# DeltaNet preparation with its mask additions on VectorE, two Gb buffers, and the scan's decay masks loaded and made step by step

## The chip, the cores and the metric

The kernel runs on one core of a Trainium2 chip. The metric is the time of one execution on the device in microseconds (us); lower is better. Beside the times there is one profiled execution, whose trace has every instruction of the engines: TensorE (PE, with its weight loads PEld), VectorE (DVE), ScalarE (ACT), GpSimd (POOL), and SyncE (SP), which issues the DMA loads and stores.

## The reference, cut to what matters

One layer over 512 latent tokens and a context of 256, width 1024: attention and a gated DeltaNet side by side, both projected from one input product, merged by gates, then a gated MLP. The change is in the DeltaNet (8 heads of width 128, two directions, chunked):

```python
gam = jnp.cumsum(log_a, axis=-1)
dec = jnp.exp(jnp.where(incl, gam[..., :, None] - gam[..., None, :], -jnp.inf))
kk = jnp.einsum('bhncd,bhnsd->bhncs', k, k)
a_mat = jnp.where(strict, beta[..., :, None] * dec * kk, 0.0) + jnp.eye(GDN_CHUNK)
uw = lax.linalg.triangular_solve(a_mat, rhs, left_side=True, lower=True, unit_diagonal=True)
...
p = dec * jnp.einsum('bhncd,bhnsd->bhncs', q, k)
...
delta = u_c - jnp.einsum('bhcd,bhde->bhce', w_c, s)
s_new = gl_c[..., None, None] * s + jnp.einsum('bhcd,bhce->bhde', kd_c, delta)
o = jnp.einsum('bhcd,bhde->bhce', qd_c, s) + jnp.einsum('bhcs,bhse->bhce', p_c, delta)
```

The matrix `dec` is needed twice: strictly triangular, times k k^T, in the triangular system; with its diagonal, times q k^T, in the scan's output. It is always made in the same way: the cumulative decays gam are broadcast from DRAM to all partitions, a mask of large numbers is added so that the excluded half vanishes in the exponential, and ScalarE takes the exponential with the token's own gam as bias.

## The kernel before, in words

The kernel works in chunks of 128 tokens, six to a head (two of the context, four latent), and takes the heads in four pairs, p = 0 to 3. For each pair there are three parts:

- `gdn_prep(p)` (L874 to L900) loads kT, makes the scale gT, and makes NN, which holds for each of the pair's two heads (hh) six masked decay matrices of both directions: per head one load of 6 x 128 numbers to all partitions into NN (direction 0) and one into Gb (direction 1), a mask addition to each (L895 by its call of `tt`; the helper's line in the trace is L108), six exps to each on ScalarE (L120), and the addition NN + Gb. For pair 0 these additions are on VectorE, for pairs 1 to 3 on GpSimd. Gb has one buffer, so the load for the second head starts when the first head's NN + Gb is done.
- `gdn_solve` (L902) has PE multiply k by k (`pk`), VectorE multiply that into NN, transposes blocks of 32 into C and X, and runs a triangular inversion of 31 steps, each a product `prod` and an addition into R. These 62 operations are on VectorE for pair 0 and on GpSimd for pairs 1 to 3. VectorE then scales R by gT and transposes it into o_tr and o_nt. `gdn_inv` (L943) builds the full inverse TTm from these with PE, VectorE (copies Y and TTm) and GpSimd.
- `gdn_scan(p)` (L1011 to L1118) walks through six steps in both directions: PE multiplies k by the state S, VectorE makes the remainder r, PE multiplies r by TTm, VectorE copies the result to dl, ScalarE scales it to dk, PE and VectorE update S. `decay_mask(c)` makes the scan's decay matrix M of latent chunk c: four loads of 128 x 128 (64 KB, L1023), two mask additions on GpSimd of 128 x 256, four exps on ScalarE. `intra(c)`, at the end of steps 1 to 4, multiplies M by the product q k^T (`pqk`). The scan makes all four masks in one line ahead of its first step; the tag M2 has four buffers.

The solve and the inverse of pair p + 1 are interleaved with the inverse and the scan of pair p. Between these, PE works through `filler()`, the input projections, whose accumulations (`mb`) VectorE and ScalarE move out of PSUM into `t` and `co`; weights are split in two parts, `whi` on ScalarE and `wlo` on VectorE, for products in three passes. `weave` deals out so many pieces of filler per step of the DeltaNet. The order of PE's matmuls is kept as written (`keep_in_program_order` while `pinned` holds). On the other engines and in the DMA queue a scheduler sets the order: by priorities (`sooner`, `solver`, `first`, `early`) and by when an instruction's inputs and buffers are there in its own model. Each engine then carries out its instructions strictly in that order, so one that waits holds all behind it. By the scheduler's order, loads of M of pair 0, which by the code come in the scan, may stand ahead of the loads of Gb of the same pair's preparation.

Of the kernel before, what the change touches and what calls it, by code (L numbers as in the profile page):

```python
# [6 lines left out]
F32 = mybir.dt.float32  # L7
F32R = mybir.dt.float32r
AF = mybir.ActivationFunctionType
ALU = mybir.AluOpType  # L10
# [4 lines left out]
P = 128  # L15
D = 1024
# [40 lines left out]
WB = 3  # L57
P0 = 1
GL = 4
# [19 lines left out]
def hybrid_layer_body(tc, x, ctxt, xT, consts, cols, rows, w_mod1, w_mod2, w_db, w_aq, w_cm, w_pa, w_pd, w_out,  # L79
# [54 lines left out]
    with es:  # L134
# [738 lines left out]

        def gdn_prep(p, eng=G):  # L874
            kT = gq.tile([P, 2, NA], F32, name="kT", tag="kT", bufs=2)
# [13 lines left out]
            for hh in range(2):  # L889
                u = slice(6 * hh, 6 * hh + 6)  # L890
                Gb = gq.tile([P, 6, P], F32, name="Gb", tag="Gb", bufs=1)
                for d, D in ((0, NN[:, u, :]), (1, Gb)):
                    r0 = d * 48 + p * 12 + hh * 6
                    SP.dma_start(D.rearrange("p a b -> p (a b)"),
                                 gamdr[r0:r0 + 6, :].rearrange("a b -> (a b)").partition_broadcast(P))  # L895
                    tt(D, D, msk_s[d].unsqueeze(1).to_broadcast([P, 6, P]), ALU.add, eng)
                    for c in range(6):
                        act(D[:, c, :], D[:, c, :], AF.Exp, scale=-1.0, bias=gam[:, r0 + c:r0 + c + 1])
                tt(NN[:, u, :], NN[:, u, :], Gb, ALU.add, eng)
            return [kT, gT, NN]  # L900
# [110 lines left out]
        def gdn_scan(p, pre, seqs):  # L1011
# [7 lines left out]
            def decay_mask(c):  # L1019
                M2 = gpool[0].tile([P, 2, 2, P], F32, name="M2", tag="M2", bufs=4)  # L1020
                for d in range(2):
                    for hh in range(2):
                        SP.dma_start(M2[:, d, hh, :], gamdr[cidx(d, hh, c), :].partition_broadcast(P))  # L1023
                    tt(M2[:, d], M2[:, d], msk_i[d].unsqueeze(1).to_broadcast([P, 2, P]), ALU.add, G)
                    for hh in range(2):
                        kc = cidx(d, hh, c)
                        act(M2[:, d, hh, :], M2[:, d, hh, :], AF.Exp, bias=ngam[:, kc:kc + 1])
# [10 lines left out]

            masks = {c: decay_mask(c) for c in (4, 3, 5, 2)}
            PTs = {}  # L1040
            for st in range(6):
                lat = st >= 2
                if st == 2:
                    oacc = gpool[0].tile([P, 2, 4, P], F32, name="oacc", tag="oacc")
# [138 lines left out]
        with early():  # L1183
            pre = gdn_prep(0, V if P0 else G)
        pas_es, y_es, yt = ExitStack(), ExitStack(), []
# [398 lines left out]
```

## Time and profile before

| | us |
|---|---|
| median of 3 runs | 1303.81 |
| lowest and highest | 1303.12, 1305.67 |
| profiled execution | 1306.96 |
| its span | 1304.3 |

The span is the time from the first to the last instruction of the profiled execution, whose own time is 2.7 us longer. Busy times are given as shares of the span, TensorE's granted clock as a share of full speed (0.978 over the span). A row of the timeline gives the start and the duration of an instruction (or of several like it in a row, with xcount), its engine, line, operation and tiles (out<-in), and in square brackets the idle time of the engine just before and what ended it. A row of the groups by line gives the count, the busy time, the mean duration in ns and the idle time before them. Preparation, solve and scan of the four pairs lie between 350 and 850 us of the span: pair 0's preparation at 350 to 412, scan 0 beside solve 1 at 460 to 545, scan 1 beside solve 2 at 560 to 640, scan 2 beside solve 3 at 640 to 725, scan 3 at 745 to 850.

### The profile page before, as it was taken

What the parts mean: (1) busy time and instruction counts of PE and PEld (TensorE: products, weight loads), DVE (VectorE), ACT (ScalarE), POOL (GpSimd) and SP (SyncE); (2) the same over time, 40 slices, a digit from 0 to 9 for tenths busy, and PEclk for the clock granted to TensorE, in tenths of its full rate; (3) what the DMA queues carried; (4) which work ended last, traced back from release to release, by engine and by line L of the source; (5) the groups of instructions that cost most, each with busy time, mean ns of one, the idle gap of its engine ahead of it and who ended that gap; (6) DMA issues with size and microseconds to landing.
All of it is one profiled execution on the core that took longest, in us unless ns stands there. A gap on an engine that the chain in (4) does not pass through costs nothing.

```text
span 1304.3 us, 20850 instructions
## 1 busy us (share of the span) xinstructions
PE 1229.6 (94%) x7835; PEld 1031.3 (79%) x7835; DVE 848.4 (65%) x1625; ACT 626.3 (48%) x1403; POOL 308.3 (24%) x364
## 2 busy tenths in 40 slices
PE   7899999999968999899998999999999999999997
PEld 4487878999857877778787878788988888888886
DVE  5886987777759986685665556555576666663323
ACT  5453656666576665474453443233354444443221
POOL 1752420000143249559447300000000000000000
PEclk8999999999998999899999999999999999999998
DMA  8656631121373342543533555265043222233331
GB/s 321 227 169 197 223 118 62 65 86 50 111 252 105 124 140 91 177 131 110 178 120 116 170 165 168 92 219 190 9 129 97 97 97 95 91 94 97 90 100 65
DMA packets 70789, 170.80 MB, mean 131 GB/s; under 512 B 7872, under 2 KB 18720, under 8 KB 69280
## 3 DMA queue, kind: packets, MB, share of 16 engines
q1 hardware_dynamic: 70688, 169.47, 39.4%
q8 instruction: 61, 1.00, 0.3%
q14 instruction: 40, 0.33, 0.1%
HBM read 144.23 MB, written 25.21 MB: 130 GB/s over the span
## 4 chain that ended last, share of the span: by engine, by line
PE 66%; POOL 10%; DVE 9%; DMA 5%; ACT 4%; issue 3%; SPq 0%; POOLq 0%; DVEq 0%; ACTq 0%
PE mc L87 32%; PE mb L87 17%; PE pq L87 4%; POOL R L108 4%; POOL prod L108 4%; PE pb L87 3%; PE pS L87 3%; PE ab L87 2%; PE ab L91 1%; DMA Gb<-gamdr 1%; PE xb L91 1%; DVE wlo L108 1%; PE pk L87 1%; DMA sz<-gdr 1%; POOL NN L108 1%
## 5 line engine op out<-in xcount | busy, mean ns | idle before, releaser
L108 DVE TENSOR_TENSOR wlo<-wraw,whi 128x1024 fp32r<-128x1024 f32 x152 | 187.6, 1235 | 162.6 <-ACT whi L120 161.6
L120 ACT ACTIVATE whi<-wraw 128x1024 fp32r<-128x1024 f32 x152 | 159.1, 1048 | 205.5 <-PE mc L87 106.5
L87 PE MATMUL mb<-hxH,whi 128*128 128x512 f32 x384 | 165.1, 430 | 2.1 <-DVE R L108 1.9
L87 PE MATMUL mb<-hxL,whi 128*128 128x512 f32 x384 | 155.0, 404 | 0.0
L87 PE MATMUL mb<-hxH,wlo 128*128 128x512 f32 x384 | 154.3, 402 | 0.0
L87 PE MATMUL mc<-h2L,whi 128*128 128x512 f32 (+1 forms) x376 | 142.7, 379 | 0.0
L87 PE MATMUL mc<-h2H,whi 128*128 128x512 f32 (+1 forms) x376 | 142.3, 378 | 0.3 <-ACT whi L120 0.3
L87 PE MATMUL mc<-h2H,wlo 128*128 128x512 f32 (+1 forms) x376 | 140.8, 374 | 0.5 <-DVE wlo L108 0.5
L108 POOL TENSOR_TENSOR rc<-rc,mhalf 128x2 f32<-128x2 f32 x4 | 3.3, 818 | 459.4 <-DVE rc L114 459.4
L87 PEld LDWEIGHTS mb<-hxH,wlo 128*128 128x128 f32 x384 | 74.0, 193 | 18.3
L87 PEld LDWEIGHTS mb<-hxH,whi 128*128 128x128 f32 x384 | 74.6, 194 | 13.9 <-ACT t L120 2.1
L87 PEld LDWEIGHTS mb<-hxL,whi 128*128 128x128 f32 x384 | 74.6, 194 | 10.3
L87 PEld LDWEIGHTS mc<-h2H,whi 128*128 128x128 f32 x376 | 70.6, 188 | 14.9 <-ACT whi L120 0.5
L87 PEld LDWEIGHTS mc<-h2H,wlo 128*128 128x128 f32 x376 | 70.6, 188 | 14.7 <-DVE wlo L108 1.0
L87 PEld LDWEIGHTS mc<-h2L,whi 128*128 128x128 f32 x376 | 70.7, 188 | 12.2
L87 PE MATMUL mc<-aH,whi 128*128 128x512 f32 (+1 forms) x198 | 72.9, 368 | 0.6 <-DVE x L117 0.6
L87 PE MATMUL mc<-aL,whi 128*128 128x512 f32 (+1 forms) x198 | 73.0, 369 | 0.0
L87 PE MATMUL mc<-aH,wlo 128*128 128x512 f32 (+1 forms) x198 | 72.0, 364 | 0.0
L117 DVE SCALAR_TENSOR_TENSOR u<-mc,col,u 128x511 f32<-128x511 f32 x88 | 65.3, 746 | 1.4
L108 POOL TENSOR_TENSOR prod<-X,R 128x31 f32<-128x31 f32 (+15 forms) x93 | 53.5, 576 | 22.3 <-DVE X L108 15.4
L108 POOL TENSOR_TENSOR R<-R,prod 128x31 f32<-128x31 f32 (+15 forms) x93 | 57.1, 613 | 6.8
L87 PE MATMUL pq<-whi,hxH 128*128 128x256 f32 x192 | 56.6, 295 | 0.0
(354 smaller groups left out, 3078.3 us busy)
## 6 DMA issues: line engine op xcount, KB each, us to landing
wraw<-in_w_cm_dram SPq DMA_DIRECT2D x48, 512.0 KB, 3.9
wraw<-in_w_up_dram SPq DMA_DIRECT2D x44, 512.0 KB, 3.7
wmd<-in_w_mod_dram SPq DMA_DIRECT2D x64, 256.0 KB, 3.8
wm<-in_w_mod_dram SPq DMA_DIRECT2D x8, 1024.0 KB, 8.2
wraw<-in_w_down_dram SPq DMA_DIRECT2D x16, 512.0 KB, 3.5
wraw<-in_w_aq_dram SPq DMA_DIRECT2D x12, 512.0 KB, 4.8
M<-gamdr SPq DMA_DIRECT2D x64, 64.0 KB, 4.4
wraw<-in_w_pa_dram SPq DMA_DIRECT2D x8, 512.0 KB, 4.0
```

Of the source, the lines that this page charges most:

```text
L87: i = nc.tensor.matmul(*a, **k)
L91: i = nc.tensor.transpose(*a, **k)
L108: (eng or V).tensor_tensor(out=out, in0=a, in1=b, op=op)
L117: V.scalar_tensor_tensor(out=out, in0=a, scalar=s, in1=b, op0=op0, op1=op1)
L120: A.activation(out, a, f, **kw)
```

## The change

In `gdn_prep` all mask additions and NN + Gb are on VectorE, for all pairs, and Gb gets a second buffer. In `decay_mask` the loads and the two additions keep their places in the order of the code (`late_op`), and the additions are on VectorE instead of GpSimd. The scan no longer makes four masks ahead of its first step: each of its steps 0 to 3 makes one at its head, for use at the end of the step behind it.

```diff
-P0 = 1
...
-        def gdn_prep(p, eng=G):
+        def gdn_prep(p):
...
-                Gb = gq.tile([P, 6, P], F32, name="Gb", tag="Gb", bufs=1)
+                Gb = gq.tile([P, 6, P], F32, name="Gb", tag="Gb", bufs=2)
...
-                    tt(D, D, msk_s[d].unsqueeze(1).to_broadcast([P, 6, P]), ALU.add, eng)
+                    tt(D, D, msk_s[d].unsqueeze(1).to_broadcast([P, 6, P]), ALU.add)
...
-                tt(NN[:, u, :], NN[:, u, :], Gb, ALU.add, eng)
+                tt(NN[:, u, :], NN[:, u, :], Gb, ALU.add)
...
-                        SP.dma_start(M2[:, d, hh, :], gamdr[cidx(d, hh, c), :].partition_broadcast(P))
-                    tt(M2[:, d], M2[:, d], msk_i[d].unsqueeze(1).to_broadcast([P, 2, P]), ALU.add, G)
+                        late_op(SP.dma_start(M2[:, d, hh, :], gamdr[cidx(d, hh, c), :].partition_broadcast(P)))
+                    late_op(V.tensor_tensor(out=M2[:, d], in0=M2[:, d], in1=msk_i[d].unsqueeze(1).to_broadcast([P, 2, P]), op=ALU.add))
...
-            masks = {c: decay_mask(c) for c in (4, 3, 5, 2)}
-            PTs = {}
+            masks, PTs = {}, {}
+            late_op = tc.keep_in_program_order
             for st in range(6):
                 lat = st >= 2
+                if st < 4:
+                    c = (4, 3, 5, 2)[st]
+                    masks[c] = decay_mask(c)
...
-            pre = gdn_prep(0, V if P0 else G)
+            pre = gdn_prep(0)
```

PE's order of instructions stays as it is. Lines behind L58 have a number smaller by one in the changed kernel up to the scan. On SP, in the preparation of pair 0, the loads of Gb and of the scan's masks M (M_5591 to M_5624 are pair 0's four masks), wraw (weights) and parts of the projections stood so before:

```order
L1023 DMA M_5591<-gamdr 128x128 x4
L1023 DMA M_5602<-gamdr 128x128 x3
L197 DMA wraw<-in_w_cm_dram 128x1024
L1023 DMA M_5602<-gamdr 128x128
L1023 DMA M_5613<-gamdr 128x128 x3
L894 DMA Gb<-gamdr 128x768
L1023 DMA M_5613<-gamdr 128x128
L1023 DMA M_5624<-gamdr 128x128 x4
L197 DMA wraw<-in_w_cm_dram 128x1024
L305 DMA vtd_133<-co 128x768
L894 DMA Gb<-gamdr 128x768 x2
```

The loads of NN and Gb at the same place of the changed kernel, from the first one on:

```order
L893 DMA NN<-gamdr 128x768
L893 DMA Gb<-gamdr 128x768
L893 DMA NN<-gamdr 128x768
L893 DMA Gb<-gamdr 128x768
L876 DMA kT<-kTd_107 128x768
L876 DMA kT<-kTd_108 128x768
L893 DMA NN<-gamdr 128x768 x2
L304 DMA ktd_126<-co 128x768
L196 DMA wraw<-in_w_cm_dram 128x1024
L893 DMA Gb<-gamdr 128x768 x4
```

The second Gb of pair 0 has moved ahead to the first; the loads of M are gone from here and stand some 20 rows further down, in the first scan, where those of all four masks of pair 0 stand close together.

VectorE's order in the same stretch, before (NN<-NN,cst and Gb<-Gb,cst are mask additions, co and t are the filler's, NN<-NN,pk is the product with k k^T):

```order
L108 TENSOR_TENSOR NN<-NN,Gb 128x768
L117 SCALAR_TENSOR_TENSOR co<-co,t_4310 128x768
L117 SCALAR_TENSOR_TENSOR t_4399<-mb,col,t_4399 128x511 x2
L108 TENSOR_TENSOR NN<-NN,pk 128x512
L108 TENSOR_TENSOR NN<-NN,pk 128x256
L108 TENSOR_TENSOR wlo<-wraw,whi 128x1024
L117 SCALAR_TENSOR_TENSOR t_4399<-mb,col,t_4399 128x255
L108 TENSOR_TENSOR Gb<-Gb,cst 128x768
L117 SCALAR_TENSOR_TENSOR t_4399<-mb,col,t_4399 128x255
L108 TENSOR_TENSOR NN<-NN,Gb 128x768
```

And in the changed kernel, from the second row on of the same place:

```order
L107 TENSOR_TENSOR NN<-NN,cst 128x768
L107 TENSOR_TENSOR g<-g,rkk_176 128x6 x2
L107 TENSOR_TENSOR NN<-NN,cst 128x768
L107 TENSOR_TENSOR NN<-NN,Gb 128x768
L116 SCALAR_TENSOR_TENSOR co<-co,t_4310 128x768
L107 TENSOR_TENSOR Gb<-Gb,cst 128x768
L116 SCALAR_TENSOR_TENSOR t_4399<-mb,col,t_4399 128x511
L107 TENSOR_TENSOR Gb<-Gb,cst 128x768
L116 SCALAR_TENSOR_TENSOR t_4399<-mb,col,t_4399 128x511
L107 TENSOR_TENSOR NN<-NN,pk 128x512
L107 TENSOR_TENSOR NN<-NN,Gb 128x768
L107 TENSOR_TENSOR NN<-NN,pk 128x256
```

Pair 1's additions to NN stand ahead of co, and its additions to Gb ahead of the product with pk; pair 0's own Gb is no longer here, being done earlier. Five to seven rows further down pair 2's two additions to Gb stand ahead of the last product with pk.

The third place is on VectorE where the solve of pair 1 begins, beside the opening of pair 0's scan (Y is a part of `gdn_inv`, C and X are the solve's). Before:

```order
L986 COPY Y_0_4243<-pb 64x384
L117 SCALAR_TENSOR_TENSOR co<-tz,mb 128x512
L108 TENSOR_TENSOR NN<-NN,pk 128x512
L986 COPY Y_1_4244<-pb 64x384
L108 TENSOR_TENSOR NN<-NN,pk 128x256
L919 STREAM_TRANSPOSE C<-NN 32x12x32 x4
L923 STREAM_TRANSPOSE X<-C 128x1024
```

And in the changed kernel:

```order
L985 COPY Y_0_4243<-pb 64x384
L116 SCALAR_TENSOR_TENSOR co<-tz,mb 128x512
L107 TENSOR_TENSOR NN<-NN,pk 128x512
L1023 TENSOR_TENSOR M_5591<-M_5591,cst 128x256
L985 COPY Y_1_4244<-pb 64x384
L107 TENSOR_TENSOR NN<-NN,pk 128x256
L1023 TENSOR_TENSOR M_5591<-M_5591,cst 128x256
L918 STREAM_TRANSPOSE C<-NN 32x12x32 x4
L1023 TENSOR_TENSOR M_5656<-M_5656,cst 128x256 x2
L922 STREAM_TRANSPOSE X<-C 128x1024
```

Four mask additions of pair 0's scan have come in between the copies of Y, C and X.

## The prediction

> **What bounds the kernel now.** The page comes first: the busy times, then the chain that ended last.
>
> ```profile
> PE 1229.6 (94%) x7835; PEld 1031.3 (79%) x7835; DVE 848.4 (65%) x1625; ACT 626.3 (48%) x1403; POOL 308.3 (24%) x364
> PE 66%; POOL 10%; DVE 9%; DMA 5%; ACT 4%; issue 3%; SPq 0%; POOLq 0%; DVEq 0%; ACTq 0%
> ```
>
> TensorE (PE) is busy for 94% of 1304.3 us; the change leaves its order of instructions as it is, so time comes and goes only in PE's waits and in its clock. The waits of PE, grouped, and two stretches by windows (window, length, then busy time of PE, PEld, DVE, ACT, POOL, PE's granted clock, DMA share, GB/s) show where waits are:
>
> ```profile
> PE pb L87 <- DVE r L117: 13.6, 7, 4.2
> 360.00:412.00 52.00, 37.42 (x198) 31.29 (x197) 39.44 (x60) 37.51 (x108) 21.98 (x17) 0.87 0.54 174
> 460.00:545.00 85.00, 77.68 (x505) 64.58 (x504) 60.88 (x117) 45.04 (x123) 60.20 (x86) 0.96 0.41 133
> ```
>
> From 360 to 412 us, where pair 0 is prepared, PE idles 52.00 − 37.42 = 14.6 us at a clock of 0.87; no other stretch that the change touches idles above 7.3 (85.00 − 77.68, pair 0's scan beside pair 1's solve). Third view: PE's timeline in the first stretch (start, duration, what, idle time before and its releaser).
>
> ```profile
> 373.61 0.66 PE L91 MATMUL xb<-cst,co 128*128 128x128 f32 x4 [2.79 <-DVE co L117]
> ...
> 390.06 1.22 PE L87 MATMUL pk<-kT 128*128 128x128 f32 x4 [8.76 <-DVE NN L108]
> ...
> 392.36 0.63 PE L87 MATMUL mb<-hxH,whi 128*128 128x512 f32 x1
> 392.78 0.63 PE L87 MATMUL mb<-hxL,whi 128*128 128x512 f32 x1
> ...
> 396.04 0.39 PE L87 MATMUL mb<-hxH,whi 128*128 128x512 f32 x1
> 396.27 0.40 PE L87 MATMUL mb<-hxL,whi 128*128 128x512 f32 x1
> ...
> 402.13 0.47 PE L87 MATMUL mb<-hxH,whi 128*128 128x512 f32 x1 [1.95 <-DVE R L108]
> ...
> 405.63 0.61 PE L87 MATMUL mb<-hxH,wlo 128*128 128x512 f32 x1
> ```
>
> Three waits, 2.79 + 8.76 + 1.95 = 13.5 us. After the long one a 512-wide matmul comes every 0.42 us (392.36 to 392.78) where it is 0.23 later (396.04 to 396.27): half speed from 390.1 to about 395.8, which costs half of 5.7, 2.9 us; after the third again, to about 406, 1.7 more. After the first there is none. What the 8.76 waits for is in the timelines of SyncE's queue (SP), VectorE (DVE), ScalarE (ACT) and GpSimd (POOL):
>
> ```profile
> 367.14 6.33 SPq L1023 DMA_DIRECT2D M<-gamdr  x7
> ...
> 374.42 1.85 SPq L1023 DMA_DIRECT2D M<-gamdr  x4
> 376.37 0.38 SPq L894 DMA_DIRECT2D Gb<-gamdr  x1
> ```
>
> ```profile
> 381.39 0.96 DVE L108 TENSOR_TENSOR Gb<-Gb,cst 128x768 f32<-128x768 f32 x1 [0.62 <-DMA Gb<-gamdr]
> ...
> 387.42 0.96 DVE L108 TENSOR_TENSOR NN<-NN,Gb 128x768 f32<-128x768 f32 x1 [4.67 <-ACT Gb L120]
> ```
>
> ```profile
> 384.94 0.69 ACT L120 ACTIVATE M<-M,ngam 128x128 f32<-128x128 f32 x2 [3.23 <-POOL M L108]
> 385.54 1.84 ACT L120 ACTIVATE Gb<-Gb,gam 128x128 f32<-128x128 f32 x6
> ```
>
> ```profile
> 384.18 2.11 POOL L108 TENSOR_TENSOR M<-M,cst 128x256 f32<-128x256 f32 x3 [3.20 <-DMA M<-gamdr]
> ```
>
> The second half's Gb has the first half's buffer and stands in SP's queue behind 11 loads of scan masks: issued at 376.37, added at 381.39. Its exps are behind two exps of scan masks, which stand 3.23 us for a GpSimd addition, itself 3.20 us behind a load. So scan masks that nobody needs before 460 hold up a Gb, hence NN+Gb, the product with pk, and PE.
>
> **The change, part by part.** The groups by line (count | busy us, mean ns | idle us before, by releaser), and the loads (count, KB, median us from issue to landing):
>
> ```profile
> L108 POOL TENSOR_TENSOR M<-M,cst 128x256 f32<-128x256 f32 x32 | 26.0, 825 | 50.9 <-DMA M<-gamdr 28.0 <-PE mb L87 22.7
> ...
> L108 POOL TENSOR_TENSOR Gb<-Gb,cst 128x768 f32<-128x768 f32 x6 | 12.6, 2093 | 19.0 <-DMA Gb<-gamdr 19.0
> ...
> L108 POOL TENSOR_TENSOR NN<-NN,Gb 128x768 f32<-128x768 f32 x6 | 11.5, 1922 | 4.8 <-ACT Gb L120 4.8
> L108 POOL TENSOR_TENSOR prod<-X,R 128x247 f32<-128x247 f32 x6 | 4.6, 762 | 0.4
> ```
>
> ```profile
> L108 DVE TENSOR_TENSOR M<-pqk,M 128x256 f32<-128x256 f32 x32 | 12.0, 417 | 9.1 <-PE pqk L87 9.1
> ...
> L108 DVE TENSOR_TENSOR NN<-NN,cst 128x768 f32<-128x768 f32 x2 | 1.9, 952 | 0.0
> ```
>
> ```profile
> M<-gamdr SPq DMA_DIRECT2D x64, 64.0 KB, 4.4
> ...
> Gb<-gamdr SPq DMA_DIRECT2D x8, 384.0 KB, 4.4
> ```
>
> Of the preparation 18 additions of about 2 us leave GpSimd for VectorE, at 0.95 each; 32 mask additions of 0.83 go too, at about 0.42 (the nearest row is the product M<-pqk,M of the same shape, since VectorE has not done this addition yet). VectorE gains 18 × 0.95 + 32 × 0.42 = 31 us of work and has 456 us free; what matters is where an addition stands in its order while its load has not landed, since all behind it stands too.
>
> *A, 350 to 412.* The loads of the second Gb come straight behind the first, the 16 loads of scan masks go behind 460, so the 8.76 goes. In its place VectorE gets eight additions of pairs 1 and 2, of 0.95 each. Carried forward by these durations (an exp is 1.84/6 = 0.31): co stands behind two of pair 1's NN additions, the PE wait of 2.79 becomes about 3.1. The first product NN<-NN,pk stands behind pair 1's two Gb additions, whose loads start when NN+Gb gives each buffer back (about 370 and 373) and land 4.4 later: two waits of some 1.0 and 1.6. The second product and the work behind C stand behind pair 2's Gb additions: 3.2 and 2.7. Sum 11.6 against 13.5, so 1.9 gained. The slow clock cost 2.9 + 1.7 = 4.6; with pieces of at most 3.2, one of which (2.79) had no slow stretch behind it and one (1.95) had, I take 1.0 to remain: 3.6 gained. A gains 5.5; the bounds are 0 (the waits for loads add up to the old ones) and 12 (of the 13.5 + 4.6 = 18.1 only the first wait and one of 3 stay).
>
> [...]
>
> *B, 460 to 545.* The scan masks of pair 0 are loaded all four at once behind 460 (only the order among late operations is kept), and the first addition stands on VectorE ahead of the copy of Y and of C, which open the scan and pair 1's solve:
>
> ```profile
> 464.79 0.56 DVE L986 COPY Y<-pb 64x384 f32<-64x384 f32 x1
> ```
>
> By 4.4 from an issue at about the same time, less what VectorE has to do meanwhile, with four additions of 0.42 and their exps, I take 2.2 lost (bounds 0 and 4.4). In the solve itself, which ends in the longest of the r waits, GpSimd is rid of two Gb additions and one NN+Gb, 2 × 2.09 + 1.92 = 6.1:
>
> ```profile
> 503.50 1.54 DVE L108 TENSOR_TENSOR wlo<-wraw,whi 128x1024 fp32r<-128x1024 f32 x1
> ```
>
> ```profile
> 504.03 1.49 POOL L108 TENSOR_TENSOR prod<-X,R 128x247 f32<-128x247 f32 x1
> ```
>
> ```profile
> 531.29 1.22 DVE L108 TENSOR_TENSOR R<-R,gT 128x1024 f32<-128x1024 f32 x1 [2.58 <-POOL R L108]
> ```
>
> ```profile
> 537.08 2.08 PE L87 MATMUL pb<-r,TTm 128*128 128x128 f32 x8 [4.19 <-DVE r L117]
> ```
>
> But an operation of GpSimd beside such a VectorE operation is held: 1.49 at 504.03, where the other five of its group average (4.6 − 1.5)/5 = 0.62, so 0.87. Six additions of pairs 2 and 3 on VectorE in this solve cost GpSimd 6 × 0.7 = 4.2 (0.7 being some 80% of it), the mask additions 0.7 more. The solve ends about 1 us sooner; R<-R,gT, which waited 2.58 for it, stands one r earlier in VectorE's order. I give PE's 4.19 back only 1.0. B loses 1.2 (−3 to +5).
>
> [...]
>
> *C, 560 to 640.* One wait here came from the same Gb:
>
> ```profile
> 586.41 1.87 ACT L120 ACTIVATE Gb<-Gb,gam 128x128 f32<-128x128 f32 x6 [3.32 <-POOL Gb L108]
> ```
>
> ```profile
> 588.83 1.98 DVE L117 SCALAR_TENSOR_TENSOR co<-co,t 128x512 f32<-128x512 f32 x1 [3.04 <-ACT co L120]
> ```
>
> ```profile
> 591.12 1.26 PE L87 MATMUL pb<-r,TTm 128*128 128x128 f32 x8 [2.23 <-DVE r L117]
> ...
> 631.87 2.08 PE L87 MATMUL pb<-dl,M 128*128 128x128 f32 x8 [2.70 <-DVE oacc L117]
> ```
>
> ScalarE stood for GpSimd's Gb, VectorE's co stood for ScalarE, r behind co, PE for r. Pair 3's Gb are made in B now, so the 2.23 goes; about 0.7 comes back by mask additions ahead of r. C gains 1.5 (0 to 2.2). The 2.70, where the second solve's transposes stand ahead of oacc, stays.
>
> *D, 640 to 725.* Two mask additions stand ahead of pair 3's X, 2 × 0.42 = 0.8, and four more beside its solve hold GpSimd by a further 0.9 or so: 1.7 lost (0 to 4).
>
> *E, 745 to 850.* The last two masks of pair 3 are loaded behind two loads of sz that take the queue 5.16 us, shortly ahead of their additions, and g_s, S and g_n stand behind these on VectorE:
>
> ```profile
> 792.67 5.16 SPq L1175 DMA_DIRECT2D sz<-gdr  x2
> ```
>
> I take 1 us for each, 2 in all (0 to 8.8, twice the 4.4).
>
> Ahead of 350 and behind 850 the order is the old one: nothing. Sum: −5.5 + 1.2 − 1.5 + 1.7 + 2.0 = −2.1. The profiled execution took 1306.96 us (span 1304.3), 3.2 above the median of the three runs; the terms are differences, which I take off the median: 1303.8 − 2.1 = **1301.7**, with 1298 to 1306 as its own range, which is about half of what the ends of B, C and D sum to (6.6 below and 7.6 above).
>
> **Rivals.** *The solves' ends move as well.* If GpSimd is held less than I think, the solve of pair 1 ends 6 us sooner and the 4.19 goes whole, with the 0.8 by which the eight matmuls behind it took longer (2.08 against 1.26) and a slow stretch as after 402.13 (1.7), 6.7; and the 2.70 in the next pair with its 0.8, 3.5. With the 1.0 that I counted taken out that is 9.2 less: 1292.5. For it: R<-R,gT did wait for GpSimd. Against it: the 1.49 beside wlo, and VectorE's 31 us of new work, most of it beside solves.
>
> *VectorE stands for the masks (slower).* GpSimd could wait 28.0 us for mask loads and cost little, having nothing else in scans 0 and 3 to do; VectorE has PE's evacuations behind every addition. If half of the 28.0 comes back on VectorE and half of that reaches PE, it is 7 us: 1308.7. It decides wherever an addition's turn comes less than 4.4 us behind its load's issue; for it speaks that masks are now made one to a step; against it, that pair 0's four are loaded together, so that only the first has to be waited for.
>
> *The first stall is only replaced.* If pairs 1 and 2's Gb loads hold VectorE as long as the masks did before, A gains 1.5 instead of 5.5: 1305.7. That the change would not do what it says hardly comes into question for Gb's buffers; "one step ahead" holds only for order, as the loads of pair 0 show.
>
> **How the numbers follow.** Chances: my sum 0.43, the solves' ends 0.20, VectorE stands for masks 0.23, the stall replaced 0.14. A measurement can tell 0.2% of this kernel, 2.6 us. Faster than 1301.2: the solves' case whole and 0.22 of my sum's, 0.42. Slower than 1306.4: VectorE's case whole, 0.05 of the replaced stall's and 0.02 of mine, 0.30. The rest, 0.28, is the same. The range is 1290 to 1311: it reaches to either outer case and 2.3 beyond, leaving out some 0.15. The likeliest case alone is 1298 to 1306.
>
> **What would show it.** Right: no wait of PE above 4 us between 374 and 400, several of 1 to 3.5 released by DVE NN, co and R, and clock 0.9 or more in that stretch; Gb loads one behind the other; the wait at 591 gone; the wait at pair 1's r still 3 to 4; new small waits behind 460 and 790 released by DVE, these standing for DMA M. Wrong: pair 1's last R above 5 us sooner relative to its first prod, and PE's r waits halved (first rival); DVE waits for DMA M summing above 10 us with PE waiting behind them (second); a clock still below 0.88 from 360 to 412 with a wait above 6 us (third).

## The result and the profile after

The changed kernel is slower: 1311.13 us median of 4 runs (1310.30 to 1311.79), beside 1304.74 of the kernel before (4 runs, 1303.12 to 1305.70). The ratio is 1.0049 (95% interval 1.0031 to 1.0067), some 6.4 us. The profiled execution took 1311.79 us (span 1310.0, granted clock 0.976), 4.8 above that of before.

The changed kernel's busy times, and the waits of PE on work of the DeltaNet's four pairs and on co (in total, times, longest):

```profile
PE 1232.6 (94%) x7835; PEld 1034.1 (79%) x7835; DVE 861.8 (66%) x1675; ACT 627.1 (48%) x1403; POOL 251.7 (19%) x314
```

```profile
PE pb L86 <- DVE r L116: 14.8, 6, 3.6
PE xb L90 <- DVE co L116: 7.7, 2, 3.9
...
PE pb L86 <- DVE dl L1081: 3.3, 1, 3.3
...
PE pb L86 <- DVE o_tr L937: 2.3, 1, 2.3
...
PE pb L86 <- DVE o_nt L939: 1.5, 1, 1.5
```

VectorE has 13 us more to do than before and GpSimd 57 less. The r waits that were to shrink have grown from 13.6 to 14.8, and three releasers on VectorE that no term spoke of (dl and the transposes o_tr, o_nt) hold PE for 3.3, 2.3 and 1.5 us.

PE has the same 7835 instructions in the same order in both kernels, so a matmul can be looked up in both traces and the difference of its start read. Between seven such matmuls, which started before at the times given:

| stage by the start before | difference at its end | in the stage | forecast |
|---|---|---|---|
| 370 to 430 (A, to the end of the preparation) | -7.8 | -7.8 | -5.5 |
| 430 to 460 (end of solve 0) | -0.8 | +7.0 | none |
| 460 to 550 (B) | +3.2 | +4.0 | +1.2 |
| 550 to 640 (C) | +3.6 | +0.4 | -1.5 |
| 640 to 741 (D) | +3.6 | 0.0 | +1.7 |
| 741 to 860 (E) | +5.5 | +1.9 | +2.0 |

In A the 8.76 is gone. PE's timeline of the changed kernel there:

```profile
374.77 1.11 PE L90 MATMUL xb<-cst,co 128*128 128x128 f32 x4 [3.90 <-DVE co L116]
...
385.22 0.71 PE L86 MATMUL pk<-kT 128*128 128x128 f32 x4 [0.60 <-DVE NN L107]
...
393.89 1.11 PE L90 MATMUL xb<-cst,co 128*128 128x128 f32 x4 [3.76 <-DVE co L116]
```

The second row is the place of the 8.76, where 0.60 is left. The third is new: 3.76 for co, which stands on VectorE behind pair 2's two additions to Gb (386.11 and 388.16) and pair 0's C. The stage gains more than forecast. But then nearly all of it is given back. The windows of the changed kernel, the second of which holds the same matmuls as the one of before under it (window, length, busy PE, PEld, DVE, ACT, POOL, PE's clock, DMA share, GB/s):

```profile
360.00:412.00 52.00, 42.46 (x231) 36.34 (x231) 42.72 (x76) 39.99 (x118) 3.19 (x4) 0.90 0.45 153
422.31:459.31 37.00, 31.96 (x334) 26.30 (x333) 30.03 (x64) 18.07 (x40) 6.43 (x12) 0.91 0.47 154
460.00:545.00 85.00, 74.06 (x484) 62.13 (x483) 63.01 (x121) 46.92 (x131) 46.17 (x68) 0.96 0.39 125
```

```profile
430.13:460.14 30.01, 28.97 (x333) 23.84 (x332) 27.87 (x54) 17.97 (x40) 6.24 (x10) 1.00 0.35 115
```

PE idles 37.00 - 31.96 = 5.0 us where it idled 1.0, and takes 3.0 longer for the same work, at a clock of 0.91 for 1.00: together the 7.0. The row of before had shown why: VectorE was busy 27.87 of 30.01 us there, since it carries solve 0. PE comes 7.8 us earlier to the solve's result, but the solve itself ends only 3.2 earlier (443.09 for 446.28), so PE is there first; before, it came late enough and did not wait. PE's timeline of the changed kernel at that place:

```profile
446.62 0.24 PE L86 MATMUL pb<-o_tr,NN 32*32 32x32 f32 x2 [2.33 <-DVE o_tr L937]
448.40 0.26 PE L86 MATMUL pb<-o_nt,NN 32*32 32x32 f32 x1 [1.54 <-DVE o_nt L939]
```

In B, PE idles 85.00 - 74.06 = 10.9 us for 7.3 before, at the same clock of 0.96. VectorE's timeline at the stage's head, and its groups over the whole span:

```profile
468.95 0.43 DVE L1023 TENSOR_TENSOR M<-M,cst 128x256 f32<-128x256 f32 x1 [3.13 <-DMA M<-gamdr]
...
471.70 0.43 DVE L1023 TENSOR_TENSOR M<-M,cst 128x256 f32<-128x256 f32 x1 [1.27 <-DMA M<-gamdr]
...
481.11 0.96 DVE L107 TENSOR_TENSOR NN<-NN,cst 128x768 f32<-128x768 f32 x1 [1.52 <-DMA NN<-gamdr]
```

```profile
L1023 DVE TENSOR_TENSOR M<-M,cst 128x256 f32<-128x256 f32 x32 | 15.5, 513 | 12.3 <-DMA M<-gamdr 12.0
L107 DVE TENSOR_TENSOR Gb<-Gb,cst 128x768 f32<-128x768 f32 x8 | 7.7, 966 | 4.0 <-DMA Gb<-gamdr 4.0
```

VectorE stands 12.0 us for loads of scan masks, 4.4 of it here (3.13 + 1.27), where 2.2 had been put down. A mask addition takes 0.51 us, not 0.42; the larger additions take 0.97, as forecast (0.95). The third row is of the preparation: VectorE stands 1.52 us for the load of pair 2's NN as well. PE waits several times in this stretch, twice so:

```profile
478.34 1.48 PE L86 MATMUL pb<-vtok,TTm 128*128 128x128 f32 x6 [1.98 <-ACT TTm L119]
...
493.45 1.26 PE L86 MATMUL pb<-r,TTm 128*128 128x128 f32 x8 [2.28 <-DVE r L116]
```

B's +4.0 is two things. From 475 to 505, where VectorE has the masks of pair 0 and six additions of pairs 2 and 3, the difference grows by 8.0 (from -0.8 to +7.2). From 505 to 550 it shrinks by 4.0, because the wait at pair 1's r, 4.19 before, is 2.40 here, with 3.4 us of slow clock behind it for 6.8.

### The profile page after: what moved, and what is told of

The parts are those of the page before. It is cut to its first block, busy times and chain, and to the rows that moved or that the text cites. A ratio compares the mean times of both kernels' runs of the same rounds, so it can differ in the third digit from the quotient of the medians.

```text
span 1310.0 us, 20829 instructions
## 1 busy us (share of the span) xinstructions
PE 1232.6 (94%) x7835; PEld 1034.1 (79%) x7835; DVE 861.8 (66%) x1675; ACT 627.1 (48%) x1403; POOL 251.7 (19%) x314
## 4 chain that ended last, share of the span: by engine, by line
PE 67%; DVE 9%; POOL 8%; DMA 4%; ACT 4%; issue 3%; SPq 1%; POOLq 0%; DVEq 0%; ACTq 0%
PE mc L86 32%; PE mb L86 18%; PE pb L86 4%; POOL R L107 4%; PE pq L86 4%; POOL prod L107 3%; PE pS L86 3%; PE ab L86 2%; PE ab L90 1%; DVE wlo L107 1%; PE xb L90 1%; DMA M<-gamdr 1%; DMA NN<-gamdr 1%; DMA gd<-tdr 1%; DMA sz<-gdr 1%
## 5 line engine op out<-in xcount | busy, mean ns | idle before, releaser
L107 POOL TENSOR_TENSOR R<-R,prod 128x31 f32<-128x31 f32 (+15 forms) x93 | 62.8, 675 | 7.1
```

Source lines behind the costliest of these rows:

```text
L107: (eng or V).tensor_tensor(out=out, in0=a, in1=b, op=op)
```

## The experiments

The theories, by their letters: **M**, the scan's masks on VectorE, which stands for their loads. **P**, the preparation's additions on VectorE. **S**, solve 0 on VectorE is the next thing late and takes A's gain away. **T**, what P costs is the time that the additions take on VectorE in the scans. **R**, what P costs is an order: the scheduler sees GpSimd with less work, expects the solve's end sooner, and puts R<-R,gT and the transposes o_tr and o_nt (1.2 + 1.9 + 1.9 us) further ahead in VectorE's order, in front of what PE is waiting for. M and P came first, S after the traces of the first runs, T and R after e8.

### e1 to e5: the parts

e1_two_gb: the kernel before with a second Gb buffer and nothing else.

```diff
-Gb = gq.tile([P, 6, P], F32, name="Gb", tag="Gb", bufs=1)
+Gb = gq.tile([P, 6, P], F32, name="Gb", tag="Gb", bufs=2)
```

> Only Gb's second buffer; all additions and masks as before. Theory M (the loss of the change comes from scan masks on VectorE, whose additions stand in order for their loads): none of that is here and the stall of 8.8 us in pair 0's preparation goes, so 2 to 6 us faster than before, about 1300. Theory P (the loss comes from the preparation's additions on VectorE, which hold GpSimd's solves): the same here, about 1300. Theory S (pair 0's solve on VectorE is the next late thing, so that most of the gain in the preparation is given back at its end): within 2 us of before.

e2_prep_on_vector: the change's gdn_prep whole, the scan's masks as before.

> The change's preparation (all its additions on VectorE, two Gb buffers); scan masks as before, all four at the scan's head, added on GpSimd. Theory M: 2 to 6 us faster than before, like the kernel with two Gb buffers alone. Theory P: slower than before by 3 us or more, most of the 6.4 that the whole change lost. Theory S: within 2 us of before, the gain of the preparation gone by 452 us.

e3_masks_on_vector: the change's decay_mask and scan (late_op, additions on VectorE, one mask to a step); gdn_prep as before, with one Gb.

> The change's scan masks (one per step, in the order of the code, added on VectorE); preparation as before, with its additions on GpSimd for pairs 1 to 3 and one Gb buffer. Theory M: slower than before by 5 us or more, VectorE idle over 10 us for mask loads. Theory P: within 2 us of before or faster, since GpSimd's solves are not held by more VectorE work than before. Theory S says nothing of the scans; in the preparation the scan's loads no longer stand ahead of Gb, which shortens the 8.8 us stall to 3 to 5.

e4_masks_on_gpsimd: the whole change, but the mask additions of the scan on GpSimd.

```diff
-late_op(V.tensor_tensor(out=M2[:, d], ...
+late_op(G.tensor_tensor(out=M2[:, d], ...
```

> The whole change, but the scan masks' additions on GpSimd again (loads still one mask per step, in the order of the code). Theory M: 1302 to 1306, since GpSimd and not VectorE stands for the loads; VectorE's idle time for mask loads, 12.0 us in the changed kernel, is 0. But GpSimd's solve of the next pair then stands for them, which may cost up to 4. Theory P: 1309 to 1312, as the whole change.

e5_two_gb_masks_on_vector: e1 and e3 together.

> Two Gb buffers and the change's scan masks on VectorE; the preparation's additions stay on GpSimd for pairs 1 to 3. It is the whole change without the move of the preparation. Theory P (the loss comes from the preparation's additions on VectorE): faster than before by about as much as two buffers alone, 1298 to 1302. Theory M (VectorE standing for mask loads costs, and e3 hid it behind the gain in the preparation): slower than with two buffers alone by 3 us or more, 1303 to 1308.

| kernel | us | before | ratio | 95% interval |
|---|---|---|---|---|
| e1 two Gb | 1300.26 | 1304.15 | 0.9973 | 0.9962 to 0.9983 |
| e2 preparation on VectorE | 1310.04 | 1304.15 | 1.0053 | 1.0040 to 1.0066 |
| e3 masks on VectorE | 1301.89 | 1304.15 | 0.9981 | 0.9971 to 0.9992 |
| e4 change, masks on GpSimd | 1344.03 | 1304.15 | 1.0313 | 1.0300 to 1.0327 |
| e5 two Gb, masks on VectorE | 1305.01 | 1304.05 | 1.0005 | 0.9994 to 1.0016 |

Two buffers alone are faster than either kernel: this is the best version found. The preparation without any change to the masks (e2) is as slow as the whole change, and the masks alone (e3) are faster than the kernel before: the loss does not need M, although VectorE did stand for DMA M in e3 as well (9.2 us). What it needs is P: the change without P is e5, 5.7 us faster than the whole (1.0005 against 1.0049). e1 and e3 remove the same stall in A, one by the buffer and one by taking the masks out of SP's queue, so e5 gains it once only and pays for the masks: 0.32% over e1, 4.2 us. Next to the moved preparation that price isn't to be seen (1.0049 against 1.0053). The costs don't add up.

e4 shows what the masks' move was needed for, once they are made step by step. Waits of PE and of ScalarE, and GpSimd's timeline:

```profile
PE pqk L86 <- DVE M L107: 38.8, 2, 20.5
```

```profile
ACT M L119 <- POOL M L1023: 55.7, 18, 15.6
```

```profile
523.40 0.25 POOL L107 TENSOR_TENSOR R<-R,prod 128x31 f32<-128x31 f32 x1
523.61 3.75 POOL L1023 TENSOR_TENSOR M<-M,cst 128x256 f32<-128x256 f32 x4
```

On GpSimd the additions stand behind the whole solve of the next pair, and the scan behind them.

### e6, e12: solve 0 (theory S)

e6_half_solve_0: e1, with pair 0's inversion cut to 16 of its 31 steps.

```diff
-for j in range(31):
+for j in range(31 if eng is G else 16):
```

> Two Gb buffers, preparation and masks as before, and pair 0's triangular inversion on VectorE cut to 16 of its 31 steps (the other 15 are left out). Theory S (the end of pair 0's solve takes back most of what the preparation gains): the waits for o_tr and o_nt, 2.8 and 1.5 us in e1, go, with the slow clock behind them, and TensorE is still 8 us or more ahead of before at the products of the inverse: 1292 to 1297 in all. Rival: what follows is late by its own inputs (the scan, the load of its tensors), the lead is lost within 20 us all the same: 1299 to 1301.

Measured 1297.90 us, ratio 0.9955 (0.9943 to 0.9968): 0.18% or 2.4 us below e1, with intervals that overlap. e1's own trace gives back as much as the change does, -10.6 us at 430 and -3.2 at 460 against before. PE's timeline at solve 0's end in e1, and in e6 what came instead:

```profile
444.85 0.31 PE L87 MATMUL pb<-o_tr,NN 32*32 32x32 f32 x2 [2.82 <-DVE o_tr L938]
```

```profile
427.05 0.48 PE L87 MATMUL mb<-hxH,whi 128*128 128x512 f32 x1 [2.87 <-DVE t L117]
```

With half the solve the wait for o_tr is gone and one of 2.87 for another result of VectorE stands earlier; e6 is -9.9 at 430 and still only -4.8 at 460. So S names the place, and the solve's length is a part of it: VectorE as a whole is what is late there. Nor is all of the gain bound to go there: e7 (below) comes to this place later than e1, -8.1 at 430, and leaves it earlier, -5.8 at 460. Its wait at the solve's end is 1.4, and no slow clock follows; in e1 the waits there are 2.8 and 1.5, and the clock is at 0.50 from 444.70 to 451.50.

e12_solve_0_on_gpsimd: e7 (below), with solve 0 on GpSimd.

```diff
-SPOOL = [int(c) for c in '123']
+SPOOL = [int(c) for c in '0123']
```

> e7 (two Gb buffers, pair 1's preparation on VectorE) with pair 0's triangular inversion on GpSimd instead of VectorE. Theory S (the end of pair 0's solve limits the gain of the preparation, and e6 bounds what it holds back at about 2.4 us): GpSimd needs about 41 us for a solve that nothing holds up, VectorE some 45 here with the filler's work between; 1298 to 1301. Rival (GpSimd is held by VectorE's wlo and additions, and the solve ends later): 1302 to 1308.

Measured 1305.77, ratio 1.0007 (0.9996 to 1.0018), 0.27% above e7. GpSimd takes 50.8 us for it, where VectorE took 44.6 in e7, and PE's wait at the end grows:

```profile
452.10 0.31 PE L87 MATMUL pb<-o_tr,NN 32*32 32x32 f32 x2 [4.46 <-DVE o_tr L938]
```

### e7 to e10: which additions cost

All on e1. e7_pair_1_on_vector and e8_pairs_2_3_on_vector split by pair; e9 moves only the mask additions of pairs 2 and 3, e10 only the sums NN + Gb.

```diff
-pre = gdn_prep(p + 1) if p + 1 < NP else None
+pre = gdn_prep(p + 1, V if p == 0 else G) if p + 1 < NP else None    (e7)
+pre = gdn_prep(p + 1, G if p == 0 else V) if p + 1 < NP else None    (e8)
...
-tt(D, D, msk_s[d].unsqueeze(1).to_broadcast([P, 6, P]), ALU.add, eng)
+tt(D, D, msk_s[d].unsqueeze(1).to_broadcast([P, 6, P]), ALU.add, V if p > 1 else eng)    (e9)
...
-tt(NN[:, u, :], NN[:, u, :], Gb, ALU.add, eng)
+tt(NN[:, u, :], NN[:, u, :], Gb, ALU.add, V if p > 1 else eng)    (e10)
```

> Two Gb buffers; pair 1's additions of the preparation on VectorE, those of pairs 2 and 3 on GpSimd; masks as before. Pair 1's stand in VectorE's order beside pair 0's preparation and ahead of its solve. Theory S with P: this is where the loss starts, pair 0's solve begins and ends later: 1303 to 1306. Rival (the loss comes beside the scans, where pairs 2 and 3 are prepared): as with two buffers alone, 1299 to 1302.

> Two Gb buffers; the additions of pairs 2 and 3 on VectorE, those of pair 1 on GpSimd; masks as before. The other half of e7's question: if the loss comes beside the scans and solves of pairs 0 and 1, 1305 to 1310; if it starts in pair 0's preparation and solve, 1299 to 1303.

> Two Gb buffers; of pairs 2 and 3 only the eight mask additions of the preparation on VectorE, NN + Gb stays on GpSimd; scan masks as before. Theory T (each addition costs by its time on VectorE, in front of t, S and r): about two thirds of the 8 us by which e8 lies above e1, 1304 to 1306. Theory R (the loss comes from R<-R,gT and the two transposes behind it, 5.2 us together, which move ahead in VectorE's order once GpSimd has less to do): here pair 1's R has moved, 1302 to 1305. The two are told apart by e10.

> Two Gb buffers; of pairs 2 and 3 only the four NN + Gb on VectorE, the mask additions stay on GpSimd; scan masks as before. Theory T: a third of e8's loss, 1301 to 1304. Theory R: two solves' R<-R,gT have moved ahead, as much as or more than e9: 1304 to 1308.

| kernel | us | before | ratio | 95% interval |
|---|---|---|---|---|
| e7 pair 1 | 1300.83 | 1304.05 | 0.9980 | 0.9969 to 0.9992 |
| e8 pairs 2 and 3 | 1308.30 | 1304.05 | 1.0034 | 1.0022 to 1.0046 |
| e9 their 8 mask additions | 1304.24 | 1304.02 | 1.0005 | 0.9996 to 1.0013 |
| e10 their 4 sums | 1304.96 | 1304.02 | 1.0010 | 1.0001 to 1.0019 |

Pair 1's additions, in A, cost nothing that can be told from e1. Those of pairs 2 and 3, beside the scans, cost 0.61% over e1, 8.0 us, which is most of the 0.76% (10.0 us) by which the change lies above e1. Eight additions (e9) and four (e10) cost about the same, 0.32 and 0.37%, though the four are half the work. The windows of e1 and of e8 from 545 to 645:

```profile
545.00:645.00 100.00, 94.89 (x888) 80.31 (x887) 65.09 (x135) 54.51 (x151) 64.34 (x94) 1.00 0.41 141
```

```profile
545.00:645.00 100.00, 91.59 (x756) 77.74 (x755) 67.14 (x140) 49.57 (x135) 54.27 (x86) 0.95 0.38 123
```

VectorE's busy time is 2 us more in 100, PE's idle time 3.3 more, and the clock 0.95 for 1.00. VectorE's timeline at the end of solve 2 and PE's wait there, first in e1:

```profile
617.95 1.22 DVE L108 TENSOR_TENSOR R<-R,gT 128x1024 f32<-128x1024 f32 x1 [2.99 <-POOL R L108]
619.09 0.75 DVE L1079 COPY dl<-pb 128x256 f32<-128x256 f32 x2
619.75 2.04 DVE L938 STREAM_TRANSPOSE o_tr<-R 128x1024 f32<-128x1024 f32 x1
```

```profile
619.65 0.68 PE L87 MATMUL pb<-dk,ktok 128*128 128x128 f32 x4 [2.40 <-DVE dl L1079]
```

and in e8:

```profile
623.11 1.22 DVE L108 TENSOR_TENSOR R<-R,gT 128x1024 f32<-128x1024 f32 x1 [2.52 <-POOL R L108]
...
625.39 1.90 DVE L938 STREAM_TRANSPOSE o_tr<-R 128x1024 f32<-128x1024 f32 x1
627.15 1.92 DVE L940 STREAM_TRANSPOSE o_nt<-R 128x1024 f32<-128x1024 f32 x1
628.91 0.76 DVE L1079 COPY dl<-pb 128x256 f32<-128x256 f32 x2
```

```profile
629.48 1.19 PE L87 MATMUL pb<-dk,ktok 128*128 128x128 f32 x4 [4.54 <-DVE dl L1079]
```

dl, for which PE waits, stood ahead of the transposes and stands behind them. None of the moved additions is in these rows: this is what raised R beside T.

### e11 and e13 to e16: T against R

e11_twelve_extra_adds: e1, with GpSimd's work left as it is and three more additions per head on VectorE for pairs 2 and 3, which nobody reads (T without R).

```diff
+if p > 1:
+    for _ in range(3):
+        scr = gq.tile([P, 6, P], F32, name="scr", tag="scr", bufs=1)
+        tt(scr, kT[:, hh, :].rearrange("p (a b) -> p a b", a=6), msk_s[0].unsqueeze(1).to_broadcast([P, 6, P]), ALU.add)
```

> Two Gb buffers, preparation on GpSimd as before, and twelve extra additions of the same shape on VectorE, three per head of pairs 2 and 3, of the loaded kT and a mask into a tile that nobody reads. They wait for no mask load, leave GpSimd its work and stand behind R<-R,gT of the solve beside them, which keeps its place. Theory T: 11 us more of VectorE work, 3 us or more slower than e1: 1303 to 1308. Theory R: as e1, 1299 to 1302.

e14_short_adds_gpsimd: e1, with the twelve additions of pairs 2 and 3 a sixth as wide, on GpSimd (R without T); e13_short_adds_vector: e8 with the same. Both leave out five sixths of the masks and sums of these pairs, and the exps get a constant in place of gam, so their results are not the layer's.

```diff
-tt(D, D, msk_s[d].unsqueeze(1).to_broadcast([P, 6, P]), ALU.add, eng)
+nc_ = 1 if p > 1 else 6
+tt(D[:, 0:nc_, :], D[:, 0:nc_, :], msk_s[d].unsqueeze(1).to_broadcast([P, nc_, P]), ALU.add, eng)
...
-    act(D[:, c, :], D[:, c, :], AF.Exp, scale=-1.0, bias=gam[:, r0 + c:r0 + c + 1])
-tt(NN[:, u, :], NN[:, u, :], Gb, ALU.add, eng)
+    act(D[:, c, :], D[:, c, :], AF.Exp, scale=-1e-32 if p > 1 else -1.0, bias=low if p > 1 else gam[:, r0 + c:r0 + c + 1])
+tt(NN[:, 6 * hh:6 * hh + nc_, :], NN[:, 6 * hh:6 * hh + nc_, :], Gb[:, 0:nc_, :], ALU.add, eng)
```

> e8 (two Gb buffers, additions of pairs 2 and 3 on VectorE) with each of these twelve additions cut to one sixth of its width, 128 x 128 instead of 128 x 768: the same instructions and loads, a sixth of the data, so the masks of pairs 2 and 3 are left out for the most part (their exps get other numbers, of the same count and shape). Theory T (time on VectorE): some 9 us of VectorE work are gone, so at most 3 us above e1, 1298 to 1303. Theory R (the place of R<-R,gT in VectorE's order, which is here ahead of r as well): as e8, 1306 to 1310.

> e1 (two Gb buffers, additions of pairs 1 to 3 on GpSimd) with those of pairs 2 and 3 cut to a sixth of their width in the same way. GpSimd is relieved as in e8, VectorE has nothing more to do, and R<-R,gT of pair 1's solve stands right behind r, where e8 has it. Theory T: as e1 or faster, 1296 to 1301. Theory R: as e8, 1305 to 1310.

e15_vector_adds_r_in_place: e8, with an equal addition on GpSimd behind each of the twelve, into a tile that nobody reads, so that the scheduler sees GpSimd as busy as before. e16_whole_change_r_in_place: the change with the same for pairs 1 to 3.

```diff
+if p > 1:
+    scr = gq.tile([P, 6, P], F32, name="scr", tag="scr", bufs=1)
+    tt(scr, D, msk_s[0].unsqueeze(1).to_broadcast([P, 6, P]), ALU.add, G)
...    (and the same behind NN + Gb)
```

> e8 (two Gb buffers, the twelve additions of pairs 2 and 3 on VectorE), and behind each of them an addition of the same shape on GpSimd into a tile that nobody reads, so that GpSimd has as much to do as in e1. By the order, R<-R,gT and the transposes of pair 1's solve then stand where e1 has them. Theory R: the 8 us of e8 go for the most part, 1299 to 1304. Theory T: as e8 or slower, 1306 to 1312, since VectorE's twelve additions are there in full.

> The whole change, and behind each addition of the preparation of pairs 1 to 3 the same extra addition on GpSimd. R<-R,gT of pairs 1 and 2 stands about where it stood before. Theory R: what the preparation's move costs goes, what the masks cost stays (e5, 5 us above e1), so 1302 to 1307, under the 1311 of the change. Theory T: 1310 to 1316.

| kernel | us | before | ratio | 95% interval | over e1 |
|---|---|---|---|---|---|
| e8 both | 1308.30 | 1304.05 | 1.0034 | 1.0022 to 1.0046 | 0.61% |
| e11 extra additions, R in place | 1309.10 | 1304.02 | 1.0040 | 1.0027 to 1.0052 | 0.67% |
| e14 R alone | 1308.78 | 1305.77 | 1.0027 | 1.0011 to 1.0042 | 0.54% |
| e13 R, short additions on VectorE | 1306.65 | 1305.77 | 1.0007 | 0.9993 to 1.0021 | 0.34% |
| e15 T, R in place | 1309.11 | 1304.03 | 1.0035 | 1.0019 to 1.0051 | 0.62% |
| e16 change, R in place | 1320.43 | 1304.03 | 1.0133 | 1.0116 to 1.0151 | 1.60% |

e14 shows that GpSimd's relief costs 7.0 us with nothing added on VectorE. e8 lies 0.27% (3.5 us) above e13, which has the same additions at a sixth of the width: that is some measure of what their length is worth, though the orders of the two differ. In e14 solve 2 ends with VectorE standing 4.66 us for it, and r stands behind the transposes; VectorE's timeline, and PE's:

```profile
620.47 1.23 DVE L108 TENSOR_TENSOR R<-R,gT 128x1024 f32<-128x1024 f32 x1 [4.66 <-POOL R L108]
...
622.28 1.90 DVE L941 STREAM_TRANSPOSE o_tr<-R 128x1024 f32<-128x1024 f32 x1
624.03 1.96 DVE L943 STREAM_TRANSPOSE o_nt<-R 128x1024 f32<-128x1024 f32 x1
625.79 1.14 DVE L117 SCALAR_TENSOR_TENSOR r<-pb,eg,vtok 128x128 f32<-128x128 f32 x4
```

```profile
626.24 2.07 PE L87 MATMUL pb<-r,TTm 128*128 128x128 f32 x8 [5.79 <-DVE r L117]
```

e11 isn't a clean run of T. R<-R,gT and dl stand one behind the other as in e1, but the added additions stand at 535 to 547 and 638 to 646, at the ends of scans 0 and 1, where e8 has its own at 469 to 482 and 574 to 583 (and two in A). And the first of the second group stands for the load of kT, ahead of oacc, which PE waits for. VectorE's group, this row of its timeline, and one wait of PE:

```profile
L108 DVE TENSOR_TENSOR scr<-kT,cst 128x768 f32<-128x768 f32 x12 | 12.8, 1070 | 2.6 <-DMA kT<-kTd 2.6
```

```profile
637.60 1.25 DVE L108 TENSOR_TENSOR scr<-kT,cst 128x768 f32<-128x768 f32 x1 [2.59 <-DMA kT<-kTd]
```

```profile
642.88 0.24 PE L87 MATMUL pb<-o_nt,NN 32*32 32x32 f32 x2 [1.35 <-DVE oacc L117]
```

So e11 shows that twelve additions can cost 8.7 us, not what those of e8 cost at their places. Matmuls looked up in the same way in e1 and in these runs tell where each loses against e1 (us; one execution of each, so that steps of 1 us say little):

| stage by the start before | change | e2 | e8 | e14 | e11 |
|---|---|---|---|---|---|
| up to 460 | 2.4 | 2.3 | 1.1 | 1.4 | 2.0 |
| 460 to 505 (head of scan 0) | 7.1 | 2.0 | 1.5 | 0.4 | 0.5 |
| 505 to 550 (end of solve 1) | -1.2 | 2.7 | 3.9 | 4.3 | -0.4 |
| 550 to 610 | 2.1 | 0.0 | 1.2 | 0.9 | 2.7 |
| 610 to 640 (end of solve 2) | 1.4 | 3.3 | 2.5 | 4.6 | 0.3 |
| 640 to 860 | 0.2 | -1.8 | -2.8 | -1.7 | 3.7 |

In e2, e8 and e14 most of the loss lies at the ends of the two solves, R's places; e11, which leaves R in place, loses nothing there. At the end of solve 2 the order is seen as well: in these three and in the changed kernel o_tr and o_nt stand ahead of the dl or r that PE waits for, in e1 and e11 behind dl. At the end of solve 1 it isn't as plain: e1 has the transposes ahead of r, too, and waits 3.75 there, and which of the orders costs what stays open. The stages in which e8 has its additions, 460 to 505 and 550 to 610, lose 2.7 together.

The whole change loses elsewhere: 7.1 of 12.0 at the head of scan 0, where P alone (e2) loses 2.0 and M alone (e5) 3.8, and next to nothing at the solves' ends. It is as slow as e2, but for the most part not by R. That PE, late from the scan's head, then finds the solve's result there would explain why the costs don't add up; no run tests it.

e15 isn't a clean run of T either, since GpSimd's added additions hold VectorE's in turn; VectorE's timeline, and GpSimd's at that time:

```profile
483.67 1.99 DVE L108 TENSOR_TENSOR Gb<-Gb,cst 128x768 f32<-128x768 f32 x1 [1.94 <-DMA Gb<-gamdr]
```

```profile
483.04 1.80 POOL L108 TENSOR_TENSOR scr<-NN,cst 128x768 f32<-128x768 f32 x1
```

GpSimd's addition ended at 484.84, 1.17 us into VectorE's 1.99, and VectorE's 0.82 behind that; the six mask additions to Gb take 1.19 us on the mean in e15 and 0.97 in e8. That also bears on e16, which is 0.84% above the change: putting R back by work on GpSimd costs more than it brings. No run has the additions on VectorE at their usual price and R in its old place, so how T and R share e8's 8.0 us is known only from the stages.

## Why the prediction was wrong, point by point

**A: right, and the gain larger.** The 8.76 went, no wait above 4 us is left between 374 and 400, and the clock from 360 to 412 is 0.90. The waits came out as two long ones (3.90 and 3.76, both for co) rather than five small ones, and two smaller waits of before, 0.84 at 411.29 and 1.52 at 422.18, went too. 5.5 was forecast, 7.8 measured, inside the bounds. The step on the slow clock (1.0 to remain) was too kind: 3.90 and 3.76 were each followed by a half-speed stretch, in windows 5.1 us at 0.53 and 2.8 at 0.51, together some 3.8 lost:

```profile
374.80:379.90 5.10, 5.10 (x26) 5.10 (x27) 3.24 (x4) 5.10 (x20) 0.00 (x0) 0.53 0.27 77
393.90:396.70 2.80, 2.80 (x14) 2.80 (x15) 1.81 (x3) 2.67 (x7) 0.00 (x0) 0.51 0.00 0
```

**The step that failed first: A's gain was carried to the end.** The sum had nothing between 412 and 460. There 7.0 of the 7.8 came back (7.4 of 10.6 in e1). The work that is late next is on VectorE, busy 27.87 of 30.01 us, and the prediction asked what is late next only inside A. So the first stall with its slow clock was worth 3.5 us at the end (e1), not 5.5. Of the 7.6 us by which the stages came out above the sum, this is 4.7 (-0.8 for -5.5); B is 2.8 and C 1.9, and D and E came out 1.8 below.

**B and C: the solve's relief was sized about right; the additions had no price on VectorE.** From the first product to the last R, solve 1 takes 49.1 us (478.99 to 528.13) for 51.0 before (480.23 to 531.26): 1.9 sooner where about 1 was forecast. Three additions of GpSimd left it, in its timeline of before 1.83 + 1.80 + 2.78 = 6.4 us, so the new work on VectorE held it for 4.5 (6.3 if the two waits for loads that went as well, 1.8, are counted), where 4.2 + 0.7 was forecast. "R<-R,gT stands one r earlier" was valued as a gain of 1.0, and at the end of solve 1 it came as a gain: the 4.19 is 2.40. What failed is the head of B. The 2.2 there stood for masks alone; the six additions of pairs 2 and 3 were counted as holding GpSimd, and their time and their loads on VectorE, ahead of what PE waits for, were put at nothing. From 475 to 505 PE lost 8.0. At the end of solve 2 the sum kept an old wait and had nothing for a new order. PE's timeline of the changed kernel at the two ends:

```profile
529.70 1.19 PE L86 MATMUL pb<-r,TTm 128*128 128x128 f32 x4 [2.40 <-DVE r L116]
...
631.00 0.68 PE L86 MATMUL pb<-dk,ktok 128*128 128x128 f32 x4 [3.32 <-DVE dl L1081]
```

The wait of 2.23 at 591 did go, as forecast. In place of the 2.70 at 631.87, for oacc, stands a 3.32 for dl, which is behind o_tr and o_nt now. That relief of GpSimd can cost, and not only gain, is what e14 adds (7.0 us over e1).

The prediction had GpSimd's hold beside VectorE's additions from one overlap (0.87 beside 1.54) and put 0.7 on each addition. In e15 VectorE is held as well: 1.99 us for an addition that takes 0.97 in e8, 1.17 of them beside GpSimd's addition of 1.80. In e8 solve 1 takes 47.6 us for 50.0 in e1, though 5.5 us of additions left it: by this difference 3.2 held, beside 3.7 us of additions on VectorE, which is most of their length; in the change 4.5 to 6.3 held beside 5.8 us of large additions and 2.5 of mask additions, which is less.

**D too high, E right in size.** D cost 0.0 for 1.7, at the edge of its bounds. E cost 1.9 for 2.0, in the two waits of the changed kernel at the last masks, where before had 0.78 in all:

```profile
798.91 1.17 PE L86 MATMUL pb<-S,kT 128*128 128x128 f32 x8 [1.05 <-DVE S L116]
...
803.97 1.29 PE L86 MATMUL pb<-r,TTm 128*128 128x128 f32 x8 [1.81 <-DVE r L116]
```

**The rivals.** "VectorE stands for the masks" gave 1308.7, the nearest time. Its sign was there (12.0 us of DVE waits for DMA M, 4.4 of them at the head of scan 0 with PE waiting behind), and that stage is where the change loses most. Yet the loss doesn't need it, since e2 is as slow without it, and its price is 4.2 us where the preparation stays on GpSimd (e5 over e1), not 7: the time is near by luck in part. "The solves' ends move as well" came for a small part: solve 1 ends 1.9 sooner relative to its first product, not 5, and r waits are 14.8 for 13.6, not halved. "The first stall is only replaced" fell with A, but what it said of the total (1.5 left of A's gain) is near what 412 to 460 left of it, by another mechanism.

## What to carry to other kernels

A stall that is removed is worth what lies between it and the next thing late, so look up the next stretch: here VectorE was busy 93% of it, its result came 3.2 us earlier for PE's 7.8, and 7.0 of the gain ended there. An engine that carries out its instructions strictly in order (in e4 PE waited up to 20.5 us for masks that stood behind a whole solve on GpSimd), and whose results the bottleneck waits for, isn't free because it is idle a third of the time (VectorE, busy 66%); work put on it can cost a good part of its own length (8.7 us for 12.8 in e11, where it also waits 2.6 for a load; nothing in e7, in another stage). Relief of another engine can cost as much (7.0 in e14), when a scheduler answers with an order that puts long instructions ahead of those waited for. Try the smallest part of a change alone first: here one buffer had the whole gain (0.27%), and the rest of the change lost three times as much.

## What the runs showed of the hardware that wasn't expected

Slow clock came behind short waits more often than the 1.95 of before had led to expect. In the changed kernel the pair of waits of 2.33 and 1.54 at 447 and the single one of 2.40 at 529.70 were each followed by half speed. Windows:

```profile
447.80:454.70 6.90, 6.30 (x110) 5.56 (x111) 2.83 (x7) 2.63 (x5) 3.31 (x7) 0.51 0.11 38
529.80:533.20 3.40, 3.40 (x10) 2.87 (x11) 3.40 (x3) 1.80 (x5) 0.00 (x0) 0.50 0.01 2
```

The stretches are 6.9 and 3.4 us long; in the traces of before and of the changed kernel every stretch at half speed but the last of the execution lasts one, two or three times 3.41 us.

The length of a wait alone doesn't tell whether half speed follows: in before it followed the 1.95 and not the 2.79. Windows of 3.41 us in before: the first two lie three whole windows ahead of the place where half speed set in next (385.62), the third ends where it set in behind the 1.95, and the fourth is at half speed:

```profile
368.55:371.96 3.41, 2.28 (x13) 1.78 (x11) 3.25 (x4) 3.41 (x11) 3.41 (x2) 1.00 1.03 401
371.96:375.38 3.42, 1.77 (x15) 1.77 (x16) 3.10 (x3) 3.42 (x12) 1.42 (x2) 1.00 0.88 203
399.27:402.68 3.41, 1.46 (x11) 1.20 (x10) 3.24 (x10) 1.42 (x2) 0.43 (x1) 1.00 0.38 114
402.68:406.09 3.41, 3.41 (x11) 2.63 (x10) 3.31 (x5) 1.07 (x4) 1.82 (x1) 0.50 0.02 7
```

The 1.95 (to 402.13) lay in one of them, in which PE was 43% busy; the 2.79 (to 373.61) was shared by two, of which the emptier was 52% busy, and no half speed followed before 385.62. In the changed kernel the second wait at 447 reached into the first slow window, which was 84% busy, and a second one followed:

```profile
444.43:447.85 3.42, 0.24 (x2) 0.13 (x2) 3.26 (x3) 1.17 (x4) 2.05 (x4) 1.00 0.33 123
447.85:451.26 3.41, 2.86 (x100) 2.79 (x101) 2.09 (x6) 2.01 (x4) 3.12 (x7) 0.50 0.21 75
451.26:454.67 3.41, 3.41 (x11) 2.76 (x10) 0.69 (x1) 0.59 (x1) 0.14 (x1) 0.50 0.00 0
```

That it matters how a wait falls into such windows is the author's reading of these few rows.

So the 2.40 cost 1.7 more, half of the 3.40, and a kernel whose waits are little longer can lose much by the clock. From 350 to 870 us, e1 and e2:

```profile
350.00:870.00 520.00, 479.69 (x3633) 403.24 (x3634) 345.66 (x709) 261.39 (x676) 215.98 (x296) 0.97 0.44 149
```

```profile
350.00:870.00 520.00, 477.04 (x3601) 402.65 (x3600) 347.45 (x721) 258.46 (x673) 185.42 (x278) 0.95 0.44 147
```

PE idles 2.7 us more in e2, and the mean clock is lower by 0.02. By the granted clock PE was busy at half speed for 24.6 us here in e1 and for 38.4 in e2; half of the difference, 6.9 us, is lost by the clock. Of the 8.5 us between these two executions the larger part is clock. Between the kernel before and the changed one it is 26.1 and 31.6, 2.7 us of the 5.7.
